# A diffusion block in float32: the last modulation section moved into the second MLP matrix, its bias, gate and residual into that matrix's first and last blocks, and fourteen instead of twelve pairs of the first matrix begun early

## The chip, the cores and the metric

One NeuronCore of one Trainium2 chip. The time is the device time of one execution in microseconds (us). Five engines run beside each other, each through its own instructions in order: PE (matmul), DVE (elementwise and PSUM reads), ACT (activations, copies), POOL (elementwise, SBUF only) and SP, which here issues all DMAs.

## The reference, cut to what matters

The kernel computes one block of a diffusion backbone for 1024 latent tokens of 1024 channels: a mixer sub-layer and then an MLP. Only the MLP and the modulation that feeds it are touched:

```python
sh1, sc1, g1, sh2, sc2, g2 = split(silu(c) @ w_mod + b_mod, 6)   # six rows of 1024
...
x = x + g1 * mix
h2 = modulate(rms_norm(x, norm2_g), sh2, sc2)
x = x + g2 * (square(relu(h2 @ w1 + b1)) @ w2 + b2)              # w1 1024x4096, w2 4096x1024
```

`g2` is the last of the six modulation sections; it gates the MLP, and only the end of the kernel needs it.

## The kernel before

Every float32 operand of a matmul is split into a high and a low part in the PE's faster format (`H` by an ACT copy, `L = raw - H` on POOL), and each product is three matmuls, H·H, L·H and H·L (`mm3`, lines 143 to 145; `prod`, lines 1638 to 1640). A split of 128x1024 is thus one ACT and one POOL instruction.

**First matrix (mlp1).** A feature tile `ft` is 128 of the 4096 hidden columns; two of them make a pair `p`, 16 pairs in all. A pair's two tiles for both halves of the tokens cost seven products of 12 matmuls instead of eight, by a scheme with sums and differences of weights and inputs. Two of the seven products (`first`) need only the first half of the tokens (`B11`, `B21`). For the first `NA` pairs these are computed ahead, while the inputs of the second half (`B22`, `T1` to `T4`, made by `mod_t`, four calls) are still being built on DVE, ACT and POOL; their result `t1` goes to DRAM and is read back in `mlp1(p)`, which then does the other five products. For pairs from `NA` on, `mlp1(p)` does all seven. The squared ReLU goes to DRAM as `s_d`.

**Second matrix (mlp2).** The 32 feature tiles are taken in blocks: two blocks of one tile, then blocks of two. A block runs over 8 token tiles `t` and 2 column halves `n`: for each of these 16 outputs, three matmuls per feature tile accumulate in one PSUM buffer (six of them, `mmc`), and an engine adds the buffer to the accumulator `acc[t]` in SBUF. The first block's sums are copied by ACT (line 1746), all others added by DVE (line 1748). `s` and `w2` tiles come through rings: `wr` (three buffers of 512 KB, shared by all weight loads), `rw2` (three), and the split `sH/sL/wH/wL` (six each, three blocks of two).

**Modulation's last section** (`mod2`, lines 1246 to 1265, items 30 to 39): eight items load 128 rows of `w_mod` into `wr` and accumulate them on DVE (line 1253 or 1255, 128x1024 each); the last two add the bias row (1261) and sum over partitions by two small matmuls (1263). The row goes to DRAM and back as `g2row`, 128 copies of `g2`. The ten items stand between the pairs 1 to 5 of mlp1.

**Gate, bias, residual.** Ahead of the last three blocks, for each of the eight `acc[t]` (1024 wide): `xr = x2 + b2*g2` on POOL (1777), `acc *= g2` (1778) and `acc += xr` (1779) on DVE. The six `w2` tiles of the last three blocks are multiplied by `g2row` on DVE (1766), so that what they add is already gated.

**What sets the order.** In most of this part the tile framework orders the instructions of each engine by its own estimates and adds the semaphore waits; the early `first` products have PE's order written out. SP issues DMAs strictly in order, so a DMA that waits for a free buffer holds up all behind it.

Of the kernel before, what the change touches and what calls it, by code (L numbers as in the profile page):

```python
# [48 lines left out]
def block_kernel(ctx, tc, io, out, dbg=None):  # L49
# [41 lines left out]
    def bcast_rows(ap, n, parts=128):  # L91
        while len(ap.shape) > 1:
            ap = ap[0]
        return bass.AP(tensor=ap.tensor, offset=ap.offset, ap=[[0, parts], [1, n]])
# [24 lines left out]
    def wload(src, shape):  # L119
        raw = wp.tile([128, 1024], F32, name="wr", tag="wr", bufs=3)  # L120
        LD.dma_start(raw[:, :int(np.prod(shape))].rearrange("p (a b) -> p a b", a=shape[0]), src)
        return raw
# [1123 lines left out]
    def mod2(i, acc, row, ps):  # L1246
        sec, k = i // 10, i % 10
        c = slice((sec + 2) * 1024, (sec + 3) * 1024)
        if k < 8:
            w = wp.tile([128, 1024], F32, name="wr", tag="wr", bufs=3)  # L1250
            LD.dma_start(w, w_mod[k * 128:(k + 1) * 128, c])
            if k == 0:
                V.tensor_scalar(acc, w, sil[:, k:k + 1], None, op0=OP.mult)
            else:
                V.scalar_tensor_tensor(acc, w, sil[:, k:k + 1], acc, op0=OP.mult, op1=OP.add)
        else:
            h = slice((k - 8) * 512, (k - 7) * 512)
            if k == 8:
                w = wp.tile([128, 1024], F32, name="wr", tag="wr", bufs=3)
                LD.dma_start(w[0:1], bcast_rows(io["b_mod"][0][c], 1024, 1))  # L1260
                V.tensor_tensor(acc[0:1], acc[0:1], w[0:1], op=OP.add)
            p = ps()
            T.matmul(p[0:1, :], onec, acc[:, h], start=True, stop=True)
            S.activation(row[0:1, 0:512], p[0:1, :], AF.Copy)
            LD.dma_start(m2_d[sec][:, h], row[0:1, 0:512])
# [355 lines left out]
    out_v = out[0].rearrange("(c t) d -> t c d", t=8)  # L1621
    w1, w2 = io["w_mlp1"][0], io["w_mlp2"][0]
    NP = 16
    NA = 12
    t1_d = dr.tile([NA, 128, 512], F32, name="t1_d")
    s_d = dr.tile([32, 128, 1024], F32, name="s_d")

# [80 lines left out]
        if p in (2, 4, 6, 8):  # L1708
            mod_t(p // 2 - 1)
    man_.__exit__(None, None, None)  # L1710
    m2_todo = list(range(30, 40))
    for p in range(NP):
        mlp1(p)
        if 1 <= p < 6:
            for _ in range(2):
                mod2(m2_todo.pop(0), xs4[3], xs4[2], trc)
        if p == 5:
            LD.dma_start(g2row, bcast_rows(m2_d[3], 1024))

    def w2_src(ft):
# [9 lines left out]
    h2b_.__exit__(None, None, None)  # L1732
    mq = ctx.enter_context(pool("mq", reuse_waits="tile"))
    acc2 = [mq.tile([128, 1024], F32, name=f"acc{t}") for t in range(8)]
    gb2 = mq.tile([128, 1024], F32, name="gb2")
    LD.dma_start(gb2, bcast_rows(io["b_mlp2"], 1024))

    def mlp2(fts, tiles, first_, last_):
        for t in range(8):
            tk = slice(t * 128, (t + 1) * 128)  # L1740
            for n in range(2):
                o = slice(n * 512, (n + 1) * 512)
                ps = mmc()
                mm3(ps, [(s_[0][:, tk], s_[1][:, tk], w_[0][:, o], w_[1][:, o]) for s_, w_ in tiles])
                if first_:
                    S.activation(acc2[t][:, o], ps, AF.Copy)
                else:
                    V.tensor_tensor(acc2[t][:, o], acc2[t][:, o], ps, op=OP.add)  # L1748
                if last_ and t == 7:
                    LD.dma_start(out_v[t][:, o], acc2[t][:, o])  # L1750
            if last_ and t < 7:
                LD.dma_start(out_v[t], acc2[t])

    def mq_split(raw, nm):
        H = mq.tile([128, 1024], F32R, name=nm + "H", tag=nm + "H", bufs=6)
        L = mq.tile([128, 1024], F32R, name=nm + "L", tag=nm + "L", bufs=6)
        S.activation(H, raw, AF.Copy)  # L1757
        G.tensor_tensor(L, raw, H, op=OP.subtract)  # L1758
        return H, L

    def mlp2_tiles(ft, gate=False):
        rs = wload(s_src(ft), (1, 1024))
        rw_ = mq.tile([128, 1024], F32, name="rw2", tag="rw2", bufs=3)
        LD.dma_start(rw_.rearrange("p (a b) -> p a b", a=1), w2_src(ft))
        if gate:
            V.tensor_tensor(rw_, rw_, g2row, op=OP.mult)
        return mq_split(rs, "s"), mq_split(rw_, "w")

    BL = [[0], [1]] + [[b, b + 1] for b in range(2, 32, 2)]
    for bi, fts in enumerate(BL):  # L1770
        last_ = bi == len(BL) - 1
        tiles = pre if bi == 0 else [mlp2_tiles(ft, bi >= len(BL) - 3) for ft in fts]
        if bi == len(BL) - 3:
            for t in range(8):
                xr = mq.tile([128, 1024], F32, name="xr", tag="xr", bufs=3)
                LD.dma_start(xr, x2_d[t])
                G.tensor_tensor(xr, xr, gb2, op=OP.add)
                V.tensor_tensor(acc2[t], acc2[t], g2row, op=OP.mult)  # L1778
                V.tensor_tensor(acc2[t], acc2[t], xr, op=OP.add)  # L1779
        mlp2(fts, tiles, bi == 0, last_)  # L1780
        if bi == 4:
            G.tensor_tensor(gb2, gb2, g2row, op=OP.mult)


_INS = ["x", "c", "ctx", "c_ctx", "w_mod", "b_mod", "norm1_g", "norm2_g", "w_in", "q_norm_g", "k_norm_g",
# [24 lines left out]
```

## Time and profile before

| | us |
|---|---|
| three timed runs: lowest, median, highest | 1962.8, 1963.23, 1966.89 |
| the profiled execution | 1956.72 |
| its span, first to last instruction | 1955.0 |
| busy in the span: PE, DVE, POOL, ACT | 1843.4, 1332.1, 1019.2, 714.8 |
| early products of the first matrix (`first`) on PE | 1249.4 to about 1318 |
| second matrix on PE | 1575.95 to about 1951.4 |

All instants below are us from the span's start. A row of the timeline gives start, duration, engine, line, operation, out<-in, and in brackets how long the engine had been idle before it and what released it. Busy times count pipelined matmuls whole, so PE reads as busy while it streams without a gap, at either clock; the number of matmuls in a stretch tells how much it did.

### The profile page before, as it was taken

Reading aid. Unit: us, or ns where it says so; the run is one execution under the profiler, and the core shown is the slowest. Engines: PE = TensorE matmul, PEld = TensorE weight load, DVE = VectorE, ACT = ScalarE, POOL = GpSimd, SP = SyncE. Lnnn points to the kernel's source line nnn. Section 1 sums busy time; section 2 is a strip of 40 time slices with the busy share of each in tenths; the row PEclk is TensorE's granted clock in tenths of the full one; section 3 lists DMA queues with packets and bytes.
Section 4 is the critical chain, followed back from the end, with each engine's and each line's share of the span. In section 5 each row is a group of like instructions: output and inputs, shape, how many; then the busy total and the mean of one; then the engine's idle time right before and its main releaser. Section 6 shows DMA issues by size and latency. Waiting matters only on the chain. (4 is left out here: it accounts for less than half of the span.)

```text
span 1955.0 us, 24269 instructions
## 1 busy us (share of the span) xinstructions
PE 1843.4 (94%) x8674; PEld 1401.6 (72%) x8674; DVE 1332.1 (68%) x2232; ACT 714.8 (37%) x1088; POOL 1019.2 (52%) x592
## 2 busy tenths in 40 slices
PE   7879999999989999999989999998999989999969
PEld 4667777778777555555548777886788878888857
DVE  5989999947897777777646454596554335555794
ACT  4452222234314555555542121454344551121100
POOL 2147566623335777777785452484445466344450
PEclk9889999999999999999999999999999999999989
DMA  9321222212222000000007655356544355223312
GB/s 314 81 71 50 74 61 74 75 64 71 76 76 87 17 23 22 23 23 18 22 12 233 218 174 162 133 164 198 174 156 133 121 193 162 87 86 99 104 45 86
DMA packets 176680, 198.56 MB, mean 102 GB/s; under 512 B 28016, under 2 KB 126116, under 8 KB 176560
## 3 DMA queue, kind: packets, MB, share of 16 engines
q1 hardware_dynamic: 176560, 197.02, 31.6%
q8 instruction: 68, 1.11, 0.2%
q14 instruction: 52, 0.43, 0.1%
HBM read 153.28 MB, written 43.57 MB: 101 GB/s over the span
## 5 line engine op out<-in xcount | busy, mean ns | idle before, releaser
L1748 DVE TENSOR_TENSOR acc<-acc,mm 128x512 f32<-128x512 f32 x256 | 172.8, 686 | 145.6 <-PE mm L145 145.4
L1199 POOL TENSOR_TENSOR accP<-accP,P 128x1024 f32<-128x1024 f32 x96 | 240.9, 2509 | 20.9 <-ACT P L1181 15.7
L136 POOL TENSOR_TENSOR wL<-wr,wH 128x1024 fp32r<-128x1024 f32 (+1 forms) x58 | 135.3, 2342 | 186.5 <-ACT wH L135 184.9
L143 PE MATMUL mm<-wH,sH 128*128 128x512 f32 x496 | 193.8, 392 | 18.2 <-DVE acc L1748 16.0
L1085 DVE TENSOR_REDUCE m<-mx 128x1 f32<-128x512 f32 x240 | 154.5, 686 | 76.1 <-PE mx L1083 69.7
L1181 ACT ACTIVATE P<-sT 128x1024 f32<-128x1024 f32 x160 | 163.8, 1026 | 116.3 <-PE sT L1177 110.8
L144 PE MATMUL mm<-wL,sH 128*128 128x512 f32 x496 | 194.7, 392 | 3.5 <-POOL wL L1758 3.5
L145 PE MATMUL mm<-wH,sL 128*128 128x512 f32 x496 | 194.5, 392 | 0.0
L1194 PE MATMUL pv<-P,Vt 128*64 128x512 f32 x640 | 150.5, 600 | 0.0
L1758 POOL TENSOR_TENSOR sL<-wr,sH 128x1024 fp32r<-128x1024 f32 x31 | 77.5, 2501 | 124.4 <-ACT sH L1757 124.4
L135 ACT ACTIVATE wH<-wr 128x1024 fp32r<-128x1024 f32 (+1 forms) x62 | 62.2, 1005 | 215.8 <-PE mm L144 67.2
L143 PEld LDWEIGHTS mm<-wH,sH 128*128 128x128 f32 x496 | 93.6, 189 | 40.2 <-DVE acc L1748 18.2
L144 PEld LDWEIGHTS mm<-wL,sH 128*128 128x128 f32 x496 | 94.1, 190 | 23.4 <-POOL wL L1758 4.0
L1757 ACT ACTIVATE sH<-wr 128x1024 fp32r<-128x1024 f32 x31 | 32.7, 1054 | 210.0 <-issue 196.6
L1663 POOL TENSOR_TENSOR wL<-wr,wH 128x1024 fp32r<-128x1024 f32 x32 | 79.6, 2492 | 55.9 <-ACT wH L1662 55.9
L145 PEld LDWEIGHTS mm<-wH,sL 128*128 128x128 f32 x496 | 94.0, 189 | 19.7
L1174 PE MATMUL sT<-Q,KH 128*128 128x512 f32 x320 | 105.2, 410 | 2.2 <-ACT P L1181 2.2
L143 PE MATMUL mm<-hH,wH 128*128 128x512 f32 x248 | 101.6, 410 | 0.0
L1177 PE MATMUL sT<-Q,K 65*128 65x512 f32 x320 | 100.9, 396 | 0.0
L145 PE MATMUL mm<-hH,wL 128*128 128x512 f32 x248 | 98.6, 398 | 0.0
L144 PE MATMUL mm<-hL,wH 128*128 128x512 f32 x248 | 98.1, 396 | 0.0
L1194 PEld LDWEIGHTS pv<-P,Vt 128*64 128x64 f32 x640 | 41.7, 136 | 71.6 <-issue 62.0
(571 smaller groups left out, 4818.2 us busy)
## 6 DMA issues: line engine op xcount, KB each, us to landing
wr<-in_w_mlp_dram SPq DMA_DIRECT2D x45, 512.0 KB
wr<-in_w_in_dram SPq DMA_DIRECT2D x35, 512.0 KB
wr<-in_w_mod_dram SPq DMA_DIRECT2D x32, 512.0 KB
s_d<-r SPq DMA_DIRECT2D x64, 256.0 KB
wr<-s_d SPq DMA_DIRECT2D x32, 512.0 KB
rw<-in_w_mlp_dram SPq DMA_DIRECT2D x31, 512.0 KB
x<-in_x_dram SPq DMA_DIRECT2D x12, 512.0 KB
xt<-in_w_mod_dram SPq DMA_DIRECT2D x24, 256.0 KB
```

The lines of the kernel that those rows point to most:

```text
L136: (low or G).tensor_tensor(L[:, :n], raw[:, :n], H[:, :n], op=OP.subtract)
L143: T.matmul(ps, lH, rH, start=i == 0, stop=False)
L144: T.matmul(ps, lH, rL, start=False, stop=False)
L145: T.matmul(ps, lL, rH, start=False, stop=i == n - 1)
L1085: V.tensor_reduce(m3[:, 4 * j + t, c:c + 1], m, axis=AX.X, op=OP.max)
L1174: T.matmul(o, KH[kv][:, ks], Q1[:, j], start=True, stop=False)
L1177: T.matmul(o, K2[kv][:, ks], Q2[:, j], start=False, stop=True)
L1181: S.activation(P, sT, AF.Exp, scale=HD ** -0.5)
L1194: T.matmul(pv[64 * j:64 * j + 64, :], Vt[:, kt, kv * 64:kv * 64 + 64], P[:, j * 512:(j + 1) * 512], start=kt == 0, stop=kt == NK - 1)
L1199: G.tensor_tensor(accP, accP, P, op=OP.add)
L1663: (low or G).tensor_tensor(L[:, :n], raw[:, :n], H[:, :n], op=OP.subtract)
L1748: V.tensor_tensor(acc2[t][:, o], acc2[t][:, o], ps, op=OP.add)
```

## The change

It does six things:

1. `NA` goes from 12 to 14: two more pairs have their two early products ahead of the rest, with PE's order written out. The number of products stays the same.
2. `mod2` items 30 to 39 leave the pairs 1 to 5 of mlp1 and stand after the blocks 3 to 7 of mlp2, two each, with buffers of their own for the sum and the row.
3. The first block's PSUM read moves from ACT to DVE and adds the bias there (`acc = bb2 + psum`); `bb2`, 128 copies of `b_mlp2`, is loaded just ahead of it.
4. Feature tile 1 gets split buffers of its own (`f`, outside mlp2's ring) and is split ahead of the loop over blocks.
5. The last four feature tiles make one block (28 to 31) instead of two.
6. The gating ahead of the last three blocks goes away, with the six multiplications of `w2` tiles. In the last block each output gets, after the add, `acc *= g2row` and `acc += xr` on DVE, 512 wide; `xr` is loaded through the `rw2` ring.

```diff
-    NA = 12
+    NA = 14
...
-    m2_todo = list(range(30, 40))
     for p in range(NP):
         mlp1(p)
-        if 1 <= p < 6:
-            for _ in range(2):
-                mod2(m2_todo.pop(0), xs4[3], xs4[2], trc)
-        if p == 5:
-            LD.dma_start(g2row, bcast_rows(m2_d[3], 1024))
...
-    gb2 = mq.tile([128, 1024], F32, name="gb2")
-    LD.dma_start(gb2, bcast_rows(io["b_mlp2"], 1024))
+    bb2 = mq.tile([128, 1024], F32, name="bb2")
+    LD.dma_start(bb2, bcast_rows(io["b_mlp2"], 1024))
...
-        if gate:
-            V.tensor_tensor(rw_, rw_, g2row, op=OP.mult)
...
-    BL = [[0], [1]] + [[b, b + 1] for b in range(2, 32, 2)]
-        if bi == len(BL) - 3:
-            for t in range(8):
-                xr = mq.tile([128, 1024], F32, name="xr", tag="xr", bufs=3)
-                LD.dma_start(xr, x2_d[t])
-                G.tensor_tensor(xr, xr, gb2, op=OP.add)
-                V.tensor_tensor(acc2[t], acc2[t], g2row, op=OP.mult)
-                V.tensor_tensor(acc2[t], acc2[t], xr, op=OP.add)
+    BL = [[0], [1]] + [[b, b + 1] for b in range(2, 28, 2)] + [[28, 29, 30, 31]]
+    pre2 = [(mq_split(wload(s_src(1), (1, 1024)), "f", 2), mq_split(wload(w2_src(1), (1, 1024)), "f", 2))]
+    for bi, fts in enumerate(BL):
+        last_ = bi == NBL - 1
+        tiles = (pre, pre2)[bi] if bi < 2 else [mlp2_tiles(ft) for ft in fts]
         for t in range(8):
+            if last_:
+                xr = mq.tile([128, 1024], F32, name="rw2", tag="rw2", bufs=3)
+                LD.dma_start(xr, x2_d[t])
             for n in range(2):
                 ps = mmc()
                 mm3(ps, [...])
-                if first_:
-                    S.activation(acc2[t][:, o], ps, AF.Copy)
-                else:
-                    V.tensor_tensor(acc2[t][:, o], acc2[t][:, o], ps, op=OP.add)
+                a_ = acc2[t][:, o]
+                V.tensor_tensor(a_, a_ if bi else bb2[:, o], ps, op=OP.add)
+                if last_:
+                    V.tensor_tensor(a_, a_, g2row[:, o], op=OP.mult)
+                    V.tensor_tensor(a_, a_, xr[:, o], op=OP.add)
...
+        if 3 <= bi < 8:
+            for _ in range(2):
+                mod2(m2_todo.pop(0), m2a, m2r, trc)
+            if bi == 7:
+                LD.dma_start(g2row, bcast_rows(m2_d[3], 1024))
```

What it does to the order, at three places. First DVE, where the fourth `mod_t` (its last sums `hf`, its low parts `T2L_10853` and `T4L_10869`) meets the weight sums of the first pairs (`cs`, which wait for a load into `wr`). Before:

```order
L1688 TENSOR_TENSOR cs<-wr 128x512
L1573 TENSOR_TENSOR hf<-hf 128x512
L1689 TENSOR_TENSOR cs<-cs,wr 128x512
L1574 TENSOR_TENSOR hf<-B21H_10193,hf 128x512
L1579 TENSOR_TENSOR T2L_10853<-hf,T2H_10852 128x512
```

and with the change:

```order
L1573 TENSOR_TENSOR hf<-hf 128x512
L1574 TENSOR_TENSOR hf<-B21H_10193,hf 128x512
L1575 TENSOR_TENSOR hf<-hf,B21L_10194 128x512
L1579 TENSOR_TENSOR T2L_10853<-hf,T2H_10852 128x512
L1688 TENSOR_TENSOR cs<-wr 128x512
```

The low part that PE's first late product needs stood behind a weight sum, and so behind a load; now it stands ahead of it.

Second SP, at the passage from mlp1 to mlp2 (`s_d<-r` are the last stores of mlp1's result, `bb` the bias rows, `rw` and `wr<-s_d` the operands of mlp2, `wr<-in_w_mod_dram` modulation's items). With the change:

```order
L1648 DMA s_d<-r 128x512 x3
L1729 DMA bb_13431<-in_b_mlp_dram 128x1024
L1741 DMA rw_13609<-in_w_mlp_dram 128x1024
L121 DMA wr<-s_d 128x1024
L1741 DMA rw_13621<-in_w_mlp_dram 128x1024
L121 DMA wr<-s_d 128x1024
L1741 DMA rw_13761<-in_w_mlp_dram 128x1024
L121 DMA wr<-s_d 128x1024
L1741 DMA rw_13773<-in_w_mlp_dram 128x1024
L1251 DMA wr<-in_w_mod_dram 128x1024 x2
L121 DMA wr<-s_d 128x1024
```

The load of the bias rows keeps its place behind the last three stores, where `gb` stood before, but mlp2's first output now needs it; modulation's items stand in one ring and one queue with the operands of mlp2.

Third DVE at the second block of two (feature tiles 2 and 3), the first eight of whose 16 outputs are shown, with the items of modulation between them. With the change:

```order
L1253 TENSOR_SCALAR m2a<-wr,sil 128x1024
L1763 TENSOR_TENSOR acc_13423<-acc_13423,mm 128x512
L1255 SCALAR_TENSOR_TENSOR m2a<-wr,sil,m2a 128x1024
L1763 TENSOR_TENSOR acc_13423<-acc_13423,mm 128x512
L1763 TENSOR_TENSOR acc_13424<-acc_13424,mm 128x512
L1255 SCALAR_TENSOR_TENSOR m2a<-wr,sil,m2a 128x1024
L1763 TENSOR_TENSOR acc_13424<-acc_13424,mm 128x512
L1763 TENSOR_TENSOR acc_13425<-acc_13425,mm 128x512 x2
L1255 SCALAR_TENSOR_TENSOR m2a<-wr,sil,m2a 128x1024
L1763 TENSOR_TENSOR acc_13426<-acc_13426,mm 128x512 x2
L1763 TENSOR_TENSOR acc_13427<-acc_13427,mm 128x512
```

Six items stand among the outputs of this block, two among those of the next, and the bias item in the one after. An output behind an item waits until the item's load has landed.

## Rows read from the trace of the kernel before

**Rows 1.** Page part 1: busy time, share of the span, instructions.
```profile
PE 1843.4 (94%) x8674; PEld 1401.6 (72%) x8674; DVE 1332.1 (68%) x2232; ACT 714.8 (37%) x1088; POOL 1019.2 (52%) x592
```
**Rows 2.** Table by windows: busy us (and count) of each engine, granted clock, DMA.
```profile
core 0: us, PE busy (x) PEld busy (x) DVE busy (x) ACT busy (x) POOL busy (x), PEclk, DMA share, GB/s
1300.00:1350.00 50.00, 44.60 (x191) 35.98 (x190) 39.59 (x41) 23.79 (x37) 27.33 (x15) 0.97 0.57 186
1350.00:1400.00 50.00, 44.91 (x185) 35.44 (x184) 29.08 (x37) 19.72 (x30) 22.34 (x10) 0.97 0.59 180
1400.00:1550.00 150.00, 150.00 (x658) 122.67 (x658) 71.34 (x104) 70.73 (x105) 68.64 (x34) 1.00 0.45 143
1550.00:1600.00 50.00, 44.28 (x188) 35.81 (x187) 12.05 (x18) 29.42 (x45) 25.97 (x12) 0.97 0.52 181
1600.00:1850.00 250.00, 250.00 (x1104) 206.81 (x1103) 136.18 (x194) 49.30 (x50) 126.63 (x54) 1.00 0.33 109
1850.00:1900.00 50.00, 34.03 (x139) 26.55 (x138) 48.54 (x40) 2.95 (x3) 31.12 (x11) 0.86 0.21 69
...
1595.50:1599.50 4.00, 4.00 (x12) 3.10 (x11) 3.50 (x6) 1.06 (x1) 4.00 (x3) 0.57 0.72 252
```
**Rows 3.** Waits of PE, 1249 to 1955: total, times, longest (us).
```profile
PE mm L143 <- DVE acc L1748: 16.0, 4, 13.8
PE mm L1639 <- POOL wL L1663: 3.7, 4, 1.1
PE mm L1640 <- DVE T2L L1579: 3.6, 1, 3.6
PE mm L144 <- POOL wL L1758: 3.5, 1, 3.5
PE mm L1638 <- ACT wH L1662: 2.4, 2, 1.5
PE mm L143 <- ACT wH L1757: 2.2, 1, 2.2
```
**Rows 4.** Timeline of DVE while the eight accumulators are gated.
```profile
1848.79 2.69 DVE L1778 TENSOR_TENSOR acc<-acc,g2row 128x1024 f32<-128x1024 f32 x1
...
1890.33 1.21 DVE L1778 TENSOR_TENSOR acc<-acc,g2row 128x1024 f32<-128x1024 f32 x1
```
**Rows 5.** Waits of DVE, 1300 to 1400: total, times, longest (us).
```profile
DVE cs L1688 <- DMA wr<-in_w_mlp_dram: 13.4, 5, 4.1
DVE xs L1255 <- DMA wr<-in_w_mod_dram: 8.4, 5, 2.3
```
**Rows 6.** Timeline of DVE ahead of PE's first wait in mlp1.
```profile
1316.99 0.75 DVE L1688 TENSOR_TENSOR cs<-wr 128x512 f32<-128x512 f32 x1 [0.95 <-DMA wr<-in_w_mlp_dram]
...
1321.67 2.82 DVE L1579 TENSOR_TENSOR T2L<-hf,T2H 128x512 fp32r<-128x512 f32 x1
```
**Rows 7.** Timelines of PE, SP and POOL at the start of mlp2.
```profile
1575.95 0.39 PE L143 MATMUL mm<-wH 128*128 128x512 f32 x1
...
1580.03 0.39 PE L143 MATMUL mm<-wH 128*128 128x512 f32 x1
...
1578.73 0.39 SPq L1736 DMA_DIRECT2D gb<-in_b_mlp_dram  x1
...
1583.85 2.39 POOL L1782 TENSOR_TENSOR gb<-gb,g2row 128x1024 f32<-128x1024 f32 x1 [12.28 <-DMA gb<-in_b_mlp_dram]
```
**Rows 8.** Timelines of SP and ACT: one load and the copy that waited for it.
```profile
1594.34 0.33 SPq L1764 DMA_DIRECT2D rw<-in_w_mlp_dram  x1
...
1597.62 1.06 ACT L1757 ACTIVATE wH<-rw 128x1024 fp32r<-128x1024 f32 x1 [3.40 <-DMA rw<-in_w_mlp_dram]
```
**Rows 9.** Timelines of POOL and DVE: single operations of mlp2 and modulation.
```profile
1591.93 2.38 POOL L1758 TENSOR_TENSOR wL<-rw,wH 128x1024 fp32r<-128x1024 f32 x1
...
1345.61 1.28 DVE L1255 SCALAR_TENSOR_TENSOR xs<-wr,sil,xs 128x1024 f32<-128x1024 f32 x1 [1.14 <-DMA wr<-in_w_mod_dram]
...
1951.37 0.69 DVE L1748 TENSOR_TENSOR acc<-acc,mm 128x512 f32<-128x512 f32 x1 [0.67 <-PE mm L145]
```

More of the change, by code (lines that the diff above doesn't have):

```diff
@@ L1734, in block_kernel, with mq_split, mlp2_tiles @@
     acc2 = [mq.tile([128, 1024], F32, name=f"acc{t}") for t in range(8)]
-    gb2 = mq.tile([128, 1024], F32, name="gb2")
-    LD.dma_start(gb2, bcast_rows(io["b_mlp2"], 1024))
-    def mlp2(fts, tiles, first_, last_):
+    bb2 = mq.tile([128, 1024], F32, name="bb2")
+    LD.dma_start(bb2, bcast_rows(io["b_mlp2"], 1024))
+    def mq_split(raw, nm, bufs):
+        H = mq.tile([128, 1024], F32R, name=nm + "H", tag=nm + "H", bufs=bufs)
+        L = mq.tile([128, 1024], F32R, name=nm + "L", tag=nm + "L", bufs=bufs)
+        S.activation(H, raw, AF.Copy)
+        G.tensor_tensor(L, raw, H, op=OP.subtract)
+        return H, L
+    def mlp2_tiles(ft):
+        rs = wload(s_src(ft), (1, 1024))
+        rw_ = mq.tile([128, 1024], F32, name="rw2", tag="rw2", bufs=3)
+        LD.dma_start(rw_.rearrange("p (a b) -> p a b", a=1), w2_src(ft))
+        return mq_split(rs, "s", 6), mq_split(rw_, "w", 6)
+    BL = [[0], [1]] + [[b, b + 1] for b in range(2, 28, 2)] + [[28, 29, 30, 31]]
+    NBL = len(BL)
+    pre2 = [(mq_split(wload(s_src(1), (1, 1024)), "f", 2), mq_split(wload(w2_src(1), (1, 1024)), "f", 2))]
+    m2_todo = list(range(30, 40))
+    m2a = mq.tile([128, 1024], F32, name="m2a")
+    m2r = mq.tile([128, 512], F32, name="m2r")
+    for bi, fts in enumerate(BL):
+        last_ = bi == NBL - 1
+        tiles = (pre, pre2)[bi] if bi < 2 else [mlp2_tiles(ft) for ft in fts]
         for t in range(8):
+            if last_:
+                xr = mq.tile([128, 1024], F32, name="rw2", tag="rw2", bufs=3)
+                LD.dma_start(xr, x2_d[t])
             tk = slice(t * 128, (t + 1) * 128)
@@ L1744, in mlp2 @@
                 mm3(ps, [(s_[0][:, tk], s_[1][:, tk], w_[0][:, o], w_[1][:, o]) for s_, w_ in tiles])
-                if first_:
-                    S.activation(acc2[t][:, o], ps, AF.Copy)
-                else:
-                    V.tensor_tensor(acc2[t][:, o], acc2[t][:, o], ps, op=OP.add)
-                if last_ and t == 7:
-                    LD.dma_start(out_v[t][:, o], acc2[t][:, o])
+                a_ = acc2[t][:, o]
+                V.tensor_tensor(a_, a_ if bi else bb2[:, o], ps, op=OP.add)
@@ L1751, in mlp2 @@
+                if last_:
+                    V.tensor_tensor(a_, a_, g2row[:, o], op=OP.mult)
+                    V.tensor_tensor(a_, a_, xr[:, o], op=OP.add)
+                    if t == 7:
+                        LD.dma_start(out_v[t][:, o], a_)
             if last_ and t < 7:
                 LD.dma_start(out_v[t], acc2[t])
[L1754 to L1764, printed above, removed]
-        if gate:
-            V.tensor_tensor(rw_, rw_, g2row, op=OP.mult)
-        return mq_split(rs, "s"), mq_split(rw_, "w")
-    BL = [[0], [1]] + [[b, b + 1] for b in range(2, 32, 2)]
-    for bi, fts in enumerate(BL):
-        last_ = bi == len(BL) - 1
-        tiles = pre if bi == 0 else [mlp2_tiles(ft, bi >= len(BL) - 3) for ft in fts]
-        if bi == len(BL) - 3:
-            for t in range(8):
-                xr = mq.tile([128, 1024], F32, name="xr", tag="xr", bufs=3)
-                LD.dma_start(xr, x2_d[t])
-                G.tensor_tensor(xr, xr, gb2, op=OP.add)
-                V.tensor_tensor(acc2[t], acc2[t], g2row, op=OP.mult)
-                V.tensor_tensor(acc2[t], acc2[t], xr, op=OP.add)
-        mlp2(fts, tiles, bi == 0, last_)
-        if bi == 4:
-            G.tensor_tensor(gb2, gb2, g2row, op=OP.mult)
+        if 3 <= bi < 8:
[3 more added lines that the diff above has]
+                LD.dma_start(g2row, bcast_rows(m2_d[3], 1024))
```

## The prediction

> **What bounds the kernel now.** I read the page's busy shares first: PE is busy 94% of the span [rows 1], so time can be won only where PE stands still or streams slowly. Where that is, the table by windows tells by counting matmuls. An undisturbed stretch holds 1104 in 250 us [rows 2], 0.2264 us each, or 221 in 50 us. Around the change three stretches hold fewer:
>
> - 1300 to 1400, the start of mlp1: 191 and 185 [rows 2]. Eight of the 191 are short transposes of 0.11 us, so (221 − 183) × 0.2264 − 0.9 = 7.7 us and 36 × 0.2264 = 8.2 us are lost, **15.9 us**.
> - 1550 to 1600, the start of mlp2: 188, 33 × 0.2264 = **7.5 us** lost.
> - 1850 to 1900, where the accumulators are gated: 139, 82 × 0.2264 = **18.6 us** lost.
>
> Together 42.0 us. PE's waits name who was late [rows 3]. In mlp1 it is DVE's low part T2L (3.6 us), POOL's wL (3.7) and ACT's wH (2.4); at the start of mlp2 ACT's and POOL's splits of feature tile 1 (2.2 + 3.5); in the last stretch DVE's add (16.0). The rest of the loss is the clock: right after the second of these waits, 1595.5 to 1599.5, the granted clock is 0.57 and 12 matmuls pass where 17.7 would [rows 2], that is, most of those 4 us ran at 1.2 instead of 2.4 GHz, after PE had idled for several us. Between 1400 and 1550 mlp1 runs without a gap [rows 2]; modulation is over there for most of the time.
>
> **The change part by part.** PE's work stays: the same products and outputs, the two small matmuls only move. Each part is thus priced by the PE time it gives back or takes.
>
> *The gating goes (−18.6).* DVE needed up to 2.69 us for one of 16 instructions of 1024 columns while POOL worked beside it, and 1.21 without POOL [rows 4]; PSUM reads queued behind them. With the change nothing of this is left there. I take the whole 18.6 back. What replaces it lies in the last block: per output three DVE instructions of 512 columns, at most 3 × 0.69 = 2.1 us [rows 9], against 12 matmuls, 2.7 us. They are covered, except behind the last output: two more instructions in the tail, at most 2 × 0.69 = **+1.4 us**. If that cover goes (DVE over 2.7 us per output), 16 outputs pay the difference. The 16 PSUM reads saved by the block of four, the dropped products on w2 and the xr loads cost or give nothing on PE.
>
> *Modulation leaves mlp1, and two more pairs begin early (−15.9).* The first wait there, T2L, has a chain in the trace: DVE waited for a load before a weight sum [rows 6] and only then came to T2L. The new order puts T2L ahead of that sum, and PE needs it 48 matmuls, 10.9 us, later. The other waits come from the ring `wr`: DVE lost 13.4 us waiting for w1 and 8.4 us for modulation's rows in these 100 us [rows 5], loads that took turns in three buffers. Without modulation's eight loads the stretch should look like 1400 to 1550. I leave 0.5 us of waits; bounds 0 and all 15.9.
>
> *The bias in the first block (takes the place of the 7.5).* Feature tile 1 now has its own buffers, loaded and split early, so the old wait goes. But DVE can read the first output only when bb2 has landed, and bb2 is issued where gb was. In the trace mlp2 begins at 1575.95, gb was issued at 1578.73, and POOL, idle for 12.28 us, took it at 1583.85 [rows 7], 5.1 us after issue. PE has six PSUM buffers of 0.68 us each, until 1580.03 (the seventh output's first matmul [rows 7]). The first read would end at 1583.85 + 0.69 = 1584.5: PE stands for **4.6 us**. After so long a wait I expect the slow clock as at 1595; there (17.7 − 12) × 0.2264 = 1.3 us went in that window, and with its edges and the restart I put 2.0 us: **+6.6 us** in place of 7.5. Bounds: another load landed 3.3 us after issue [rows 8], which makes 2.7 us of wait and perhaps no slow clock; above, 8. I take the upper landing, since gb is the same load in the same place behind the same stores. The Trainium skill ("DMA: Bandwidth & Descriptors", section "Anatomy of one DMA — SWDGE (gpsimd) path") gives about 2 us fixed plus bytes over 436 GB/s. As an estimate from that page bb2 would take 3.2 us and the sum would be some 2 to 4 us better; the row of rw agrees with it, gb's does not.
>
> *Modulation inside mlp2 (+1).* DVE runs in order, so each item holds the PSUM reads behind it until its load has landed; PE goes on for six outputs of 1.36 us, 8.2 us. The critical item is the third, behind three outputs of the block of tiles 2 and 3. Its load stands on SP behind a w2 load that waits for a buffer which the split of tile 6's weight frees. Counted from the start of mlp2: POOL begins about 3.4 us in (mlp1's last activation ends before gb is issued, 2.8 us in [rows 7]; then one ACT copy) and needs 2.38 us per split [rows 9]; nine splits bring it to 24.8; tile 6's s is loaded only then (3.3 us), copied (1.06 us [rows 8]) and split, and its weight after that, to 34.0. The load lands 3.3 us later, 37.3, or some 1.3 us later still as the second of two in flight; with the item's 1.28 us [rows 9] and the read's 0.69 the buffer is free at 39.3 to 40.6. The block began at 21.8 + 6.6 = 28.4, and PE needs that buffer after nine outputs, at 40.6. So it is hidden, by next to nothing; I put 1 us for all eight items. Bounds: 0, and, when each load takes the 5.1 us of gb, waits of 2.4, 1.3, 0.8 and 1.7 us at four items, 6.2 us, with two slow stretches 9.6. Behind the block the chain is loose again: POOL has over 20 us for four splits.
>
> **Sum.** −42.0 + 1.4 + 0.5 + 6.6 + 1.0 = −32.5 us. Against the profiled execution 1956.7 − 32.5 = 1924.2. The timed median is 1963.2, 6.5 us above that execution, and I take the difference as constant: **1931 us**.
>
> **The rivals.**
>
> *The items stall PE* (the bounds just given): 6 to 10 us instead of 1, 1936 to 1940. For it: the margin of the third item is under 1.5 us, and in mlp1 these same loads held DVE 8.4 us [rows 5]. Against: mlp2 moves 109 GB/s where mlp1's start moved 180 [rows 2].
>
> *Mlp1's waits were not modulation's.* If the splits' own chain is slow at the start, 10 to 16 us stay, 1942 to 1947. For it: PE waits for wL and wH there, never directly for a modulation row. Against: the gap-free 150 us after it.
>
> *The last block becomes DVE's.* If POOL still split beside it, the two added instructions would take the double, as 2.69 against 1.21 us shows for 1024 columns [rows 4]: 0.69 + 2 × 1.35 = 3.4 us per output against 2.7, 16 × 0.7 = 11 us, 1942. The splits of tiles 30 and 31 fall in the block before, so I give it little. The Trainium skill ("GPSIMD Engine Reference", section "8. Key points") says that GpSimd shares its SBUF interfaces with VectorE and contends with instructions of two SBUF inputs; by that rule this would happen here whenever both run, and the trace agrees in rows 4.
>
> *Slower than before.* The eight items, in DVE's order, could take back all of it: that needs 32.5 / 8 = 4.1 us of PE wait at each, so each output held for over 8.2 + 4.1 = 12.3 us. It decides whether a modulation load lands later than some 10 us after DVE comes to it, because SP holds it behind a POOL split that itself waits for PE. At 5 us per item the time is 1931 + 39 = 1970. Against: in mlp1 the longest such wait was 2.3 us [rows 5].
>
> *It does not do what it says:* the freed time comes back as another wait of PE, and the total stays within 4 us of 1963.
>
> **How the numbers follow.** Forecast 0.68; stalled items 0.17; mlp1's waits stay 0.06; DVE-bound last block 0.04; slower 0.03; no difference 0.02. Two runs that differ by less than 0.2%, 3.9 us, cannot be told apart here. Faster by more takes the first four, 0.95; same 0.02; slower 0.03. The best case of the bounds, −42.0 + 1.4 + 2.7 = −37.9, gives 1925; the timed runs themselves spread by 4 us, so the range begins at 1922. Above it takes in the stalled items with a few us left in mlp1: 1943. Beyond lie parts of the last cases, under 0.15.
>
> **What would show it.** In 1300 to 1400 some 440 matmuls, no wait for T2L and none of DVE for modulation rows. At the start of mlp2 one wait of PE for DVE's add, 3 to 5 us, ended by the load of bb2, followed by a stretch of low clock. In the next 40 us DVE waits for modulation rows of 3 to 6 us without a PE wait above 1 us. From 1600 on 221 matmuls per 50 us up to the end, and three DVE instructions behind the last matmul. Wrong: a PE wait at each item, waits for wL or wH left in mlp1, or no wait for bb2.

## The result, and the profile after

| | before | after |
|---|---|---|
| timed runs: lowest, median, highest (us) | 1962.8, 1964.27, 1966.89 | 1931.89, 1934.08, 1935.68 |
| the profiled execution | 1956.72 | 1933.46 |
| its span | 1955.0 | 1931.7 |
| first product of mlp1 | 1249.4 | 1254.0 |
| from there to the end of the span | 705.6 | 677.7 |

The changed kernel takes 0.984 of the time before, 95% interval 0.983 to 0.986: 30.2 us less between the medians (four runs each; the median before was 1963.23 in the three shown above), and inside the range. The two profiled executions differ by only 23.3 us. But the first product of mlp1 comes 4.6 us later in the one after, and nothing ahead of it was changed; that instant also drifts from trace to trace of the kernels below (1250.4 to 1256.0; of the kernel before there is one trace). So the traces are compared from mlp1's first product on: 27.9 us less there, where the prediction had 32.5.

The page gives PE and DVE now:

```profile
PE 1838.1 (95%) x8674; PEld 1398.4 (72%) x8674; DVE 1315.5 (68%) x2242; ACT 705.5 (37%) x1072; POOL 989.9 (51%) x583
```

As in [rows 1], the same 8674 matmuls, in a shorter span. The table by windows (PE's busy time with its count of matmuls, the granted clock, the DMA share, GB/s) tells where the time came from:

```profile
1300.00:1350.00 50.00, 48.08 (x215) 1.00 0.56 181
1350.00:1400.00 50.00, 50.00 (x222) 1.00 0.54 163
1550.00:1600.00 50.00, 46.08 (x197) 0.97 0.60 212
1600.00:1650.00 50.00, 46.84 (x197) 0.97 0.54 179
1650.00:1850.00 200.00, 200.00 (x879) 1.00 0.30 98
1850.00:1900.00 50.00, 50.00 (x222) 1.00 0.21 73
```

Against [rows 2], the start of mlp1 has 437 matmuls instead of 376 in 100 us, and 1850 to 1900 has 222 instead of 139: both are nearly whole. A full 50 us holds 222 here. In 1300 to 1350 15 are missing, since eight of its 215 are short transposes as before (0.9 us in all), 25 in 1550 to 1600 and 25 in 1600 to 1650; at 0.2264 us that is 2.5, 5.7 and **5.7 us**. Counted directly, these stretches hold 61, 9 and 83 matmuls more than before and 25 fewer in 1600 to 1650 (222 before), 128 in all or 29.0 us. Less 1.4 us behind the last matmul that is a gain of 27.6: the 27.9 of the traces.

PE's waits from mlp1's first product to the end (total, times, longest):

```profile
PE mm L143 <- DVE acc L1763: 7.1, 4, 3.9
PE mm L1638 <- DVE r L1655: 1.9, 2, 1.2
```

Of the six groups of [rows 3] only DVE's adds are left; the small waits for DVE's rows `r` stand in mlp1, at 1326.6 and 1338.9. The four waits for DVE's adds are 3.9 us at the start of mlp2 and 2.2, 0.4 and 0.5 at modulation's items. The timeline of DVE shows what stood in front of these adds (start, duration, engine, line; in brackets the idle time before and what ended it):

```profile
1572.25 10.18 DVE L1763 TENSOR_TENSOR acc<-bb,mm 128x512 f32<-128x512 f32 x16 [6.41 <-DMA bb<-in_b_mlp_dram]
...
1593.22 0.75 DVE L1253 TENSOR_SCALAR m2a<-wr,sil 128x1024 f32<-128x1024 f32 x1
1593.98 0.69 DVE L1763 TENSOR_TENSOR acc<-acc,mm 128x512 f32<-128x512 f32 x1
1594.58 3.17 DVE L1255 SCALAR_TENSOR_TENSOR m2a<-wr,sil,m2a 128x1024 f32<-128x1024 f32 x1
1597.68 1.27 DVE L1763 TENSOR_TENSOR acc<-acc,mm 128x512 f32<-128x512 f32 x2
1605.12 1.28 DVE L1255 SCALAR_TENSOR_TENSOR m2a<-wr,sil,m2a 128x1024 f32<-128x1024 f32 x1 [6.16 <-DMA wr<-in_w_mod_dram]
1606.32 1.87 DVE L1763 TENSOR_TENSOR acc<-acc,mm 128x512 f32<-128x512 f32 x3
```

Two loads hold it: first bb2, then the row of modulation's third item. The timelines of SP and PE give their issue and the matmul that came late (mlp2's first matmul starts at 1564.83):

```profile
1567.61 0.39 SPq L1729 DMA_DIRECT2D bb<-in_b_mlp_dram  x1
...
1600.05 0.33 SPq L1741 DMA_DIRECT2D rw<-in_w_mlp_dram  x1
1600.47 0.38 SPq L1251 DMA_DIRECT2D wr<-in_w_mod_dram  x1
```
```profile
1572.99 0.50 PE L143 MATMUL mm<-wH 128*128 128x512 f32 x1 [3.92 <-DVE acc L1763]
...
1607.05 0.50 PE L143 MATMUL mm<-wH,sH 128*128 128x512 f32 x1 [2.23 <-DVE acc L1763]
```

DVE could start 4.64 us after bb2's issue, and 4.65 us after the issue of the third item's load. That load stands on SP behind a `w2` load (1600.05) that waited until the split of tile 6's weight had freed a buffer. POOL's timeline shows the splits of tile 6, first of its s, then of its weight:

```profile
1594.26 2.41 POOL L1735 TENSOR_TENSOR sL<-wr,sH 128x1024 fp32r<-128x1024 f32 x1 [2.48 <-ACT sH L1734]
1596.62 3.40 POOL L1735 TENSOR_TENSOR wL<-rw,wH 128x1024 fp32r<-128x1024 f32 x1
```

The second of them took 3.40 us instead of 2.4, and DVE's second item (1594.58 to 1597.75) 3.17 instead of 1.28: each ran in part beside the other engine's instruction.

Behind each of the two waits PE ran on at a granted clock of 0.57 for some 4 us, that is mostly at 1.2 instead of 2.4 GHz (windows of PE: 11 or 10 matmuls in 4 us, then 19):

```profile
1573.00:1577.00 4.00, 4.00 (x11) 0.57 0.97 385
1577.00:1581.00 4.00, 4.00 (x19) 1.00 0.92 330
1607.00:1611.00 4.00, 3.95 (x10) 0.57 0.81 298
1611.00:1615.00 4.00, 4.00 (x19) 1.00 0.38 123
```

So of each 5.7 us, 1.5 to 1.7 us are the clock (17.7 − 11 or − 10 matmuls).

The end is as drawn: three DVE instructions behind the last matmul, which starts at 1926.32 (timeline of DVE):

```profile
1926.74 0.69 DVE L1763 TENSOR_TENSOR acc<-acc,mm 128x512 f32<-128x512 f32 x1 [0.58 <-PE mm L145]
1927.47 0.69 DVE L1765 TENSOR_TENSOR acc<-acc,g2row 128x512 f32<-128x512 f32 x1
1928.19 0.69 DVE L1766 TENSOR_TENSOR acc<-acc,rw 128x512 f32<-128x512 f32 x1
```

Before, DVE had 0.67 us of idle time and one instruction per output there [rows 9]; now 0.58 us are left beside three, so the last block is covered, with that much to spare.

### The profile page after: what moved, and what is told of

It is laid out like the page before. It is cut to its first block, busy times and chain, and to the rows that moved or that the text cites. A ratio compares the mean times of both kernels' runs of the same rounds, so it can differ in the third digit from the quotient of the medians.

```text
span 1931.7 us, 24218 instructions
## 1 busy us (share of the span) xinstructions
PE 1838.1 (95%) x8674; PEld 1398.4 (72%) x8674; DVE 1315.5 (68%) x2242; ACT 705.5 (37%) x1072; POOL 989.9 (51%) x583
## 3 DMA queue, kind: packets, MB, share of 16 engines
q1 hardware_dynamic: 179216, 199.11, 32.5%
## 4 chain that ended last, share of the span: by engine, by line
PE 47%; issue 9%; POOL 8%; DVE 5%; DMA 2%; ACT 1%; SPq 0%; POOLq 0%; ACTq 0%; DVEq 0%
PE pv L1194 7%; PE mm L143 7%; PE mm L144 7%; PE mm L145 7%; POOL wL L1663 5%; PE sT L1174 4%; PE sT L1177 4%; PE mx L1083 3%; PE mm L1591 1%; PE mm L1592 1%; PE mm L1593 1%; PE mx L1088 1%; DMA wr<-in_w_mod_dram 1%; PE mx L1218 1%; PE mm L210 1%
## 5 line engine op out<-in xcount | busy, mean ns | idle before, releaser
L1763 DVE TENSOR_TENSOR acc<-acc,mm 128x512 f32<-128x512 f32 x240 | 162.4, 686 | 127.8 <-PE mm L145 127.8
L143 PE MATMUL mm<-wH,sH 128*128 128x512 f32 x480 | 187.8, 391 | 3.2 <-DVE acc L1763 3.2
L145 PE MATMUL mm<-wH,sL 128*128 128x512 f32 x480 | 187.5, 391 | 0.0
L144 PE MATMUL mm<-wL,sH 128*128 128x512 f32 x480 | 187.4, 390 | 0.0
L1735 POOL TENSOR_TENSOR sL<-wr,sH 128x1024 fp32r<-128x1024 f32 x30 | 72.2, 2408 | 154.2 <-ACT sH L1734 154.2
L1194 PEld LDWEIGHTS pv<-P,Vt 128*64 128x64 f32 x640 | 41.9, 137 | 72.7 <-issue 63.4
```

Source lines behind the costliest of these rows:

```text
L143: T.matmul(ps, lH, rH, start=i == 0, stop=False)
L144: T.matmul(ps, lH, rL, start=False, stop=False)
L145: T.matmul(ps, lL, rH, start=False, stop=i == n - 1)
L1194: T.matmul(pv[64 * j:64 * j + 64, :], Vt[:, kt, kv * 64:kv * 64 + 64], P[:, j * 512:(j + 1) * 512], start=kt == 0, stop=kt == NK - 1)
L1763: V.tensor_tensor(a_, a_ if bi else bb2[:, o], ps, op=OP.add)
```

## The experiments

The theory after this reading: the gain comes from three places that are independent of each other (the gating, modulation's loads in mlp1, T2L's place), and two new waits of 5.7 us each are left, for bb2 and for the third item's load. Four kernels take the new waits away, four undo one part of the change, one goes further, one repeats the changed kernel. The table shows them all; "rest" is the time from mlp1's first product to the end of the span, and the last columns count the matmuls of two stretches (222 is full).

| kernel | median us | ratio to before, 95% | rest us | 1550–1600 | 1600–1650 |
|---|---|---|---|---|---|
| before | | | 705.6 | 188 | 222 |
| the change | 1934.08 | 0.9827 to 0.9861 | 677.7 | 197 | 197 |
| again | 1932.91 | 0.9831 to 0.9866 | 677.2 | 196 | 197 |
| e_bias | 1931.11 | 0.9821 to 0.9850 | 672.9 | 223 | 191 |
| e_late | 1928.12 | 0.9798 to 0.9838 | 671.9 | 196 | 222 |
| e_biaslate | 1922.96 | 0.9781 to 0.9810 | 666.0 | 222 | 223 |
| e_biasring | 1925.72 | 0.9788 to 0.9839 | 669.3 | 222 | 209 |
| u_mod | 1939.09 | 0.9850 to 0.9880 | 681.6 | 196 | 222 |
| na12 | 1938.07 | 0.9842 to 0.9875 | 683.5 | 196 | 196 |
| u_gate | 1940.14 | 0.9863 to 0.9892 | 684.4 | 192 | 209 |
| u_pairs | 1941.86 | 0.9871 to 0.9900 | 682.9 | 192 | 208 |
| best_na16 | 1920.43 | 0.9767 to 0.9799 | 666.2 | 222 | 223 |

### The bias row early (e_bias)

```diff
+    bb2 = g2row
+    LD.dma_start(bb2, bcast_rows(io["b_mlp2"], 1024))
     for p in range(NP):
         mlp1(p)
...
-    bb2 = mq.tile([128, 1024], F32, name="bb2")
-    LD.dma_start(bb2, bcast_rows(io["b_mlp2"], 1024))
```

> The changed kernel, but the bias row of the MLP is loaded before mlp1 into the tile that later takes modulation's row (bb2 is that tile), so that it lies in SBUF long before mlp2 begins. Theory (the wait at the start of mlp2 is the landing of bb2, and the slow clock follows that wait): no PE wait for DVE's add in the first 20 us of mlp2, no low clock there, 221 instead of 197 matmuls in those 50 us: the 5.4 us lost there go, 1929 against the changed kernel's 1934. The waits at the modulation items stay or grow by a little, since PE reaches them earlier and their loads do not come earlier: then 1929 to 1932. Rival (DVE is late there for another reason, its adds or the splits of tile 1): the wait stays, 1934.

The wait and the low clock at the start of mlp2 are gone (223 matmuls), so bb2's landing was their cause. But only 4.8 us of rest are won, because the third item's load now costs more: 191 matmuls, 31 × 0.2264 = 7.0 us. Its rows, DVE's and PE's:

```profile
1606.14 1.29 DVE L1255 SCALAR_TENSOR_TENSOR m2a<-wr,sil,m2a 128x1024 f32<-128x1024 f32 x1 [9.65 <-DMA wr<-in_w_mod_dram]
...
1608.08 0.80 PE L143 MATMUL mm<-wH,sH 128*128 128x512 f32 x1 [4.56 <-DVE acc L1763]
```

DVE and PE come to that place earlier, the row does not (DVE began the item 40.9 us after the start of mlp2, 40.3 in the changed kernel): DVE waits 9.65 instead of 6.16 us for it, PE 4.56 instead of 2.23. bb2's wait had hidden a part of the next one.

### Modulation's items later (e_late)

```diff
-        if 3 <= bi < 8:
+        if 8 <= bi < 13:
             for _ in range(2):
                 mod2(m2_todo.pop(0), m2a, m2r, trc)
-            if bi == 7:
+            if bi == 12:
```

> The changed kernel, but modulation's eight items are issued five blocks later (from block 8 on, two to a block), where POOL's splits are well ahead. Theory (the items stall PE in the first 70 us of mlp2 because their loads stand on SP behind weight loads that wait for POOL's splits, which are late there): the PE waits of 2.2, 0.4 and 0.5 us go, the stretch of 50 us that had 197 matmuls has 221, and no new wait comes later: 1934 - 5 = 1929. The wait for bb2 stays. Rival 1 (any item of 1.3 to 3.3 us in DVE's order with a load of 3 to 5 us behind a shared ring of three buffers stalls PE, wherever it stands): the waits move along, 1934. Rival 2 (the ring of three is then late for the splits in the middle of mlp2): new PE waits for splits, 1934 or above.

The waits at the items go and none comes in their place: 222 matmuls, rest 5.8 us shorter, and one wait of PE for an add is left, bb2's (waits of PE in mlp2, then DVE's waits for the rows):

```profile
PE mm L143 <- DVE acc L1763: 4.2, 1, 4.2
```
```profile
DVE m2a L1255 <- DMA wr<-in_w_mod_dram: 21.8, 7, 3.8
```

DVE now waits for these rows longer than in the changed kernel, 21.8 us against 16.9, and it costs nothing: the longest single wait is 3.8 us, and with the item's 1.28 and a read's 0.69 that stays under the 8.2 us that PE can go on. That sum is not enough by itself: for the third item of the changed kernel 6.16 + 1.28 + 0.69 = 8.1 us also stay under 8.2, and PE stood still. The 8.2 us run from the moment at which PE finished the output ahead of the item. There that was 1596.66 (PE stopped at 1607.05 − 2.23 = 1604.82, six outputs later), and DVE, behind with its reads, began to wait only at 1598.96. These 2.3 us count too, and 2.3 + 8.1 − 8.2 is the wait of 2.2 us. What matters is when the row lands after that output, not how long DVE waits for it. In e_late DVE is up to date when it comes to the items. The rivals fall: items of this kind, in the shared ring, stall PE only where the row lands late after that output.

### Both (e_biaslate)

> Both edits: the bias row loaded before mlp1, and modulation's items five blocks later. Theory (two separate waits, 5.4 us each with their slow clock): they add, 1934 - 10.8 = 1923, and PE goes through mlp2 at 221 matmuls per 50 us from its first 50 us to its end. Rival (one wait hides in the other, or the time comes back as a wait for POOL's splits at the start): 1929 or above.

The two edits together. PE waits nowhere in mlp2 (table by windows of PE):

```profile
1550.00:1600.00 50.00, 50.00 (x222) 1.00 0.63 215
1600.00:1650.00 50.00, 50.00 (x223) 1.00 0.33 106
1650.00:1850.00 200.00, 200.00 (x879) 1.00 0.36 116
```

Rest 666.0, 11.7 us less than the change, against 4.8 + 5.8 = 10.6 for the two alone; by the median 1923, as expected. This kernel beats both.

### The ring or the place (e_biasring)

```diff
-            w = wp.tile([128, 1024], F32, name="wr", tag="wr", bufs=3)
+            w = mq.tile([128, 1024], F32, name="mw", tag="mw", bufs=2)
             LD.dma_start(w, w_mod[k * 128:(k + 1) * 128, c])
```

with the same for the bias row of modulation, in mlp2 alone, and with the bias row of the MLP early; the items stay in the early blocks.

> The bias row loaded before mlp1, modulation's items where the change puts them, but their loads in a ring of two buffers of their own, not in the ring of three that the feature tiles use. It tells whether the shared ring or the place of the items makes their waits. If the ring does: the first items find their rows there, no PE wait at the items, 1923 to 1925. If it is SP's order (the loads from the third on still stand behind weight loads that wait for POOL's splits) or DVE's time at the items: waits of 1 to 4 us stay, 1927 to 1931.

DVE's waits for the rows fall to 2.0 us in all, PE's to 1.7 in three (DVE's groups in 1560 to 1700, then waits of PE):

```profile
L1255 DVE SCALAR_TENSOR_TENSOR m2a<-mw,sil,m2a 128x1024 f32<-128x1024 f32 x7 | 16.4, 2339 | 2.0 <-DMA mw<-in_w_mod_dram 2.0
```
```profile
PE mm L143 <- DVE acc L1763: 1.7, 3, 1.1
```

So the shared ring made most of the wait: against e_bias 3.6 us of rest are won, 18 matmuls in that stretch. What is left is mainly DVE's own time: five of the seven items take 2.2 to 3.5 us beside POOL's splits, the two others 1.28 us while POOL is idle. The run does not rule out SP's order as a cause beside the ring. With two buffers of the shared ring no longer held by items, tile 6's s is loaded 17.7 us after the start of mlp2 instead of 24.6, POOL's splits come earlier, and the third item's load goes out after 27.7 us instead of 35.6. So the ring acted, in part at least, through the loads that stood ahead on SP. The median, 1925.7, lies between the two expected, but the five runs spread from 1919.9 to 1934.0, so the reading rests on the trace.

### Modulation back in mlp1 (u_mod)

The ten items go back between the pairs 1 to 5, on `xs4`, and `g2row` is loaded at pair 5; fourteen early pairs stay.

> The changed kernel, but modulation's last section goes back into pairs 1 to 5 of mlp1, as before; fourteen early pairs, the bias and the new ending stay. Measure: the time from mlp1's first product to the end of the span, 677.7 us in the changed kernel, 705.6 before. Theory (modulation's loads in the ring of three buffers make most of mlp1's waits): mlp1 loses some 8 to 12 of its 15.9 us again (the wait for T2L, 3.6 us, stays away, since with fourteen early pairs T2L still stands ahead of the weight sums), the 5.4 us at the items in mlp2 go: 677.7 + 10 - 5.4 = 682, 1938. Rival (the two more early pairs made the gain, by T2L's place and by the time they give the splits): mlp1 keeps its gain, 677.7 - 5.4 = 672, 1929.

Rest 681.6 against 682 expected. The table by windows and PE's waits in mlp1:

```profile
1300.00:1350.00 50.00, 48.41 (x216) 1.00 0.64 205
1350.00:1400.00 50.00, 44.49 (x190) 1.00 0.62 195
1400.00:1550.00 150.00, 148.39 (x647) 1.00 0.48 151
```
```profile
PE mm L1639 <- POOL wL L1663: 3.4, 4, 0.9
PE mm L1638 <- DVE r L1655: 3.3, 3, 1.7
PE mm L1638 <- ACT wH L1662: 2.0, 3, 0.8
```

Against the changed kernel (215, 222, 663) 47 matmuls are missing, 10.6 us. The waits for wL and wH are those of [rows 3] again; the one for T2L is not there. In mlp2 the 5.7 us at the items go. The run puts modulation's loads and its DVE instructions back together, so it does not separate the ring from DVE's time. DVE's own waits for loads of w1 do not tell it either: 13.4 us in 1300 to 1400 before [rows 5], 17.5 here, 20.1 in the changed kernel, where PE waits for no split. What speaks for the ring is SP's timeline: here a modulation load goes out about 2 us ahead of a pair's first load of w1 (1354.76 and 1356.79, 1370.40 and 1372.59), and from pair to pair these loads of w1 stand 16.7 us apart (1339.36 to 1389.35, three steps), 13.7 us in the changed kernel (1343.34 to 1384.54).

### Twelve early pairs (na12)

```diff
-    NA = 14
+    NA = 12
```

> The changed kernel with twelve pairs begun early instead of fourteen: T2L's last tile then stands behind two weight sums on DVE, as before, while modulation stays out of mlp1. Theory (modulation's loads were the cause of DVE's waits, and the order of T2L only mattered because of them): T2L may wait a little, 0 to 4 us with its restart, 1934 to 1938. Rival (twelve pairs give the splits too little time): waits for wL and wH come back, 10 us or more, 1944 and above.

22 matmuls fewer than the change in 1300 to 1350, 5.0 us, at a granted clock of 0.93; rest 5.8 us longer. That is above the 0 to 4 expected, but PE waits for no split of weights, so it isn't the rival: what is late there is DVE's chain. The timeline of DVE:

```profile
1322.07 1.29 DVE L1688 TENSOR_TENSOR cs<-wr 128x512 f32<-128x512 f32 x1 [1.67 <-DMA wr<-in_w_mlp_dram]
1323.28 1.77 DVE L1573 TENSOR_TENSOR hf<-hf 128x512 f32<-128x512 f32 x1
1324.97 0.68 DVE L1689 TENSOR_TENSOR cs<-cs,wr 128x512 f32<-128x512 f32 x1
1325.58 0.68 DVE L1574 TENSOR_TENSOR hf<-B21H,hf 128x512 f32<-128x512 f32 x1
1326.18 0.68 DVE L1579 TENSOR_TENSOR T2L<-hf,T2H 128x512 fp32r<-128x512 f32 x1
1326.78 2.85 DVE L1575 TENSOR_TENSOR hf<-hf,B21L 128x512 f32<-128x512 f32 x1
1329.55 0.74 DVE L1655 SCALAR_TENSOR_TENSOR r<-mm,cols,t 128x512 f32<-128x512 f32 x1
```

DVE waits 1.67 us for a load of w1 and does two weight sums inside the chain that makes T2L and the row r behind it. PE waits 0.7 us for T2H, 0.4 for T2L and 2.9 for r, and the clock falls. No load of modulation is near. Most of PE's wait is thus for `r`, not for T2L; and twelve pairs also bring PE there some 12 us earlier than fourteen (first matmul on T2H 69.0 us after mlp1's first product, 80.9 in the changed kernel), which this run does not separate from DVE's order. So the two early pairs pay 5 us by themselves, and the two parts, 10.6 + 5.0 us, more than account for the 13.8 us that mlp1 won (61 matmuls).

### The gating back (u_gate)

```diff
+        if bi == NBL - 3:
+            for t in range(8):
+                xr = mq.tile([128, 1024], F32, name="rw2", tag="rw2", bufs=3)
+                LD.dma_start(xr, x2_d[t])
+                V.tensor_tensor(acc2[t], acc2[t], g2row, op=OP.mult)
+                V.tensor_tensor(acc2[t], acc2[t], xr, op=OP.add)
```

and the multiplications of the last `w2` tiles, blocks of two, and one add per output in the last block.

> The changed kernel with the gating put back where it was: three blocks before the end DVE multiplies each accumulator by modulation's row and adds x, 16 instructions of 1024 columns, the last three blocks' weights are multiplied on DVE, the last block is one of two tiles, and its outputs need no more than the add. The bias is in the first block, so POOL adds nothing to x, which is the only difference to before there. Theory (the stall is DVE's 16 instructions, 1.2 us each alone and up to 2.7 beside POOL's splits, ahead of the PSUM reads): it comes back nearly whole, 12 to 18 us, less 1.4 of tail: 1934 + 14 = 1948, with a wait of PE for DVE's add of over 8 us near 1850. Rival (POOL's own 16 additions to x made it): only 3 to 6 us come back, 1938.

In between: 1850 to 1900 has 178 matmuls, 44 × 0.2264 = 10.0 us lost where it was 18.6 before. (POOL's additions before were 8 of 1024 columns; the text on record says 16.) PE's waits at the end, and DVE's two groups of this kernel:

```profile
PE mm L143 <- DVE acc L1768: 5.0, 1, 5.0
PE mm L144 <- POOL wL L1735: 1.5, 1, 1.5
```
```profile
L1759 DVE TENSOR_TENSOR acc<-acc,g2row 128x1024 f32<-128x1024 f32 x8 | 13.3, 1670 | 0.0
L1760 DVE TENSOR_TENSOR acc<-acc,rw 128x1024 f32<-128x1024 f32 x8 | 11.2, 1412 | 0.0
```

The same 16 instructions took 19.0 + 17.5 = 36.5 us in the kernel before and take 24.5 here: 12 us less of DVE, 8.6 us less of PE. So about half of the stall was the 16 instructions ahead of the PSUM reads, and the other half came with POOL's work beside them, which made them longer. From the first to the last of the 16 POOL was busy 32.3 of 44.5 us before, with five additions (14.2 us) and six splits, and 8.2 of 32.6 us here, with splits alone: x comes through the ring of `w2`, and most splits fall later. What part the additions had and what part the splits, this run does not separate. Neither theory as written holds.

### Blocks of two up to the end (u_pairs)

```diff
-    BL = [[0], [1]] + [[b, b + 1] for b in range(2, 28, 2)] + [[28, 29, 30, 31]]
+    BL = [[0], [1]] + [[b, b + 1] for b in range(2, 32, 2)]
```

> The changed kernel with blocks of two feature tiles up to the end instead of one block of four. Each output of the last block is then 6 matmuls, 1.36 us, against three DVE instructions of 0.69 us, 2.1 us. Theory (the block of four is what covers the new ending): DVE sets the pace of the last 16 outputs, 33 us against 22, and the end comes 9 to 11 us later: 1944. Rival (six PSUM buffers and the idle time of DVE before cover it): 1934 to 1937.

7.8 us slower than the change by the median: the block of four does cover the new ending. PE is done earlier than DVE (last matmul and last DVE instruction of this kernel):

```profile
1926.81 0.39 PE L145 MATMUL mm<-wH,sL 128*128 128x512 f32 x1
```
```profile
1935.35 0.69 DVE L1766 TENSOR_TENSOR acc<-acc,rw 128x512 f32<-128x512 f32 x1
```

DVE ends 9.2 us after that matmul's start; in the changed kernel it was 2.6 (1928.88 − 1926.32), so 6.7 us are lost. The 9 to 11 expected took 0.69 us for each instruction; back to back they start every 0.60 us (as from 1325.58 on in the rows of na12), so three need 1.8 us per output.

### Sixteen early pairs, and the change again (best_na16, again)

> The kernel with both edits (bias row early, modulation's items five blocks later), and all sixteen pairs begun early instead of fourteen. From mlp1's first product to the end that kernel took 666.0 us; 1.7 us of PE waits are left in it, for DVE's activation rows r while T1 to T4 are formed. Theory (these rows stand on DVE behind the last T tiles, and what made them late is the order that twelve or fourteen pairs already moved): two more pairs change nothing but the place, 665 to 666, 1922 to 1923. Rival (each pair begun early gives the splits more time): the 1.7 us go, 664, 1921. Against both: two more rows of products go through the memory and back, which could make mlp1's end late, 1926.

Rest 666.2 against 666.0: nothing. The median is 2.5 us below that of e_biaslate, but the intervals of the two overlap, and the traces do not show that difference behind mlp1's start. A wait of PE of 1.4 us for `r` is left, and one of 0.3 for an add.

> The changed kernel once more, unchanged, for the spread of its own waits from run to run. Theory (the two waits belong to the program, their size to the run): a wait of 3.5 to 4.5 us for bb2 with 25 to 30 matmuls fewer than 222 in those 50 us, and at the items 13 to 31 fewer, as seen in the runs that share this part; 1934. Rival (the items' waits in the first profile were an accident): no loss at the items, 1929.

The waits come again: 4.0 us for bb2, 2.4 at the third item, 196 and 197 matmuls. They belong to the program. Their size moves with small things: in u_pairs and u_gate, whose mlp2 starts in the same order, 208 and 209 matmuls pass in the stretch of the items. In u_pairs the wait of PE at the third item is 0.94 us, and the clock stays at 1.00 behind it (timeline of PE, then the window of the 4 us behind):

```profile
1608.87 0.50 PE L143 MATMUL mm<-wH,sH 128*128 128x512 f32 x1 [0.94 <-DVE acc L1763]
```
```profile
1608.90:1612.90 4.00, 4.00 (x18) 1.00 0.91 278
```

Its start of mlp2 lost more (192 matmuls): behind the wait for bb2, 3.81 us, the granted clock was 0.50 in the first 4 us and 0.78 in the next, where the changed kernel was back at 1.00. So PE wanted the buffer of the third item 40.9 us after the start of mlp2 instead of 40.0, and it was free after 41.9 instead of 42.2.

## Why the prediction was right, and where it was off

The time, 1934.08, lies in the range, 3.1 us above the forecast. Part of that closeness is luck: behind mlp1's start the traces show 27.9 us where the sum had 32.5, 4.6 us apart, and the medians happen to differ by 2.3 us more than the traces. By its own steps:

- **The gating (−18.6): right.** No wait of PE is left between 1650 and the end; 222 matmuls in 1850 to 1900. The reason given, DVE's instructions lengthened by POOL ahead of the PSUM reads, is borne out by u_gate: with far less of POOL's work beside them, 10.0 us come back, not 18.6. (The 2.69 us given as the most is the first of the 16; the longest took 3.36.)
- **The tail (+1.4): right.** Two DVE instructions more, from 1927.47 to 1928.88.
- **mlp1 (−15.9, 0.5 left): right in the main, 2.5 us left.** Both parts named pay by themselves: modulation's place 10.6 us (u_mod), the two early pairs 5.0 us (na12). That modulation cost by its loads in the ring, and not by its time on DVE, is argued and not shown. What is left are two waits for DVE's rows `r`, 1.9 us in all. (By the step's own terms the rival with 10 to 16 us left comes to some 1940 to 1946, not 1942 to 1947.)
- **bb2 (+6.6): right, 5.7 us**, and 5.7 to 6.8 in the runs that share it. The wait was 3.9 us instead of 4.6 (4.5 by the step's own rows, 1584.54 − 1580.03), mostly since DVE could read 4.64 us after the issue, not 5.1. The sentence that drew on the Trainium skill ("DMA: Bandwidth & Descriptors", section "Anatomy of one DMA — SWDGE (gpsimd) path") gave an estimate of 3.2 us; that section's fit is for DMAs issued by GpSimd (POOL), and this load, issued by SP with the stores ahead of it, took 4.64, so the estimate does not carry over here.
- **Modulation's items in mlp2 (+1.0): this step failed; 5.7 us.** The critical place was right, the third item, and so was the chain behind its load. The step put the load's issue 34.0 us after the start of mlp2 and its landing 3.3 to 4.6 us later. It was issued after 35.6 us and DVE began after 40.3, so the buffer came free 42.2 us in, where PE wanted it after 40.0 (0.6 us earlier than in the step, as bb2 had cost less). Two terms of the sum were too short. The split of tile 6's weight, which frees the buffer that SP waited for, ran beside DVE's second item and took 3.40 us, not 2.38; with 0.4 us for the issue of the w2 load ahead that is most of the 1.6 us by which the load went out late. And the load took 4.65 us, not the 3.3 of the forecast. The second item itself, 3.17 us instead of 1.28, made nothing later on DVE, which waited 6.16 us behind it. The clock, 1.7 us, was counted only in the upper bound. The rival *the items stall PE* is what happened in this part, a little below its 6 to 10 us, at one item mostly. The sign set for this step, no PE wait above 1 us there, failed with it.
- **The offset of 6.5 us: not constant.** The profiled execution before was 6.5 us below its median then, the one after 0.6. Between the medians the gain is 30.2 us, behind mlp1's start in the traces 27.9.

The other rivals fell: mlp1's waits went with modulation and with the place of T2L and the rows behind it; the last block keeps 0.58 us of DVE idle per output, and POOL has no instruction at all from 1880 on; no item held an output for 12 us. But u_gate and e_biasring show that the rule behind the third rival is at work here. DVE's instructions of 1024 columns took 2.39 and 2.20 us on average with much of POOL's work beside them and 1.67 and 1.41 with little, and the items of e_biasring 2.2 to 3.5 beside POOL's splits and 1.28 without. The Trainium skill ("GPSIMD Engine Reference", section "8. Key points") states this contention for instructions with two SBUF inputs; the trace agrees. In the step on the items it was left out, and there it cost about 1 us, the longer split ahead of the third item's load.

## What to carry to other kernels

When a load into a shared ring holds an in-order engine, ask for each wait how long the engine behind it can go on, here 8.2 us from the end of the output ahead: eight waits of up to 3.8 us, begun soon after that output, cost nothing; one of 6.2 us, begun 2.3 us after it, stopped PE. A constant row that the first instruction of a stage needs is loaded a stage ahead, into a tile that is not yet in use: that and a later place for the items gave 11 us more than the change alone. And a wait that is taken away hands part of its time to the next one, so remove neighbouring waits together.

## What the runs showed of the hardware that was not expected

How long PE waits does not settle by itself what the clock does. In the changed kernel the granted clock fell to 0.57 for some 4 us behind waits of 2.23 and 3.92 us, so the shorter of them cost 1.7 us more; it stayed at 1.00 behind waits of 0.94 us (u_pairs) and 1.10 us (e_biasring). But in the kernel before it was still 1.00 in the 4 us behind a wait of 2.19 us (to 1589.18), although PE soon stopped again, and fell to 0.58 behind two of only 1.45 and 0.85 us that came close together (to 1379.20 and 1380.55), while two of 1.74 and 0.85 us as close in u_mod (to 1387.30 and 1388.65) left it at 1.00. Nor does the length set how long the clock stays low: behind 3.92 us it was back within 4 us, behind 3.81 us in u_pairs only after some 6. Which activity decides it, these runs do not show. POOL pays for the contention too: its split beside DVE's second item took 3.40 us in place of 2.4, and that made the load late which stood behind it on SP.
